# A down projection of seven half-size block products in place of eight

## The chip, the cores and the metric

One core of a Trainium2 chip runs one layer of a transformer-like trunk for 512 tokens. The metric is the time of the kernel on the device, in microseconds (us). Engines are named by what they do and by their short names in the profile: TensorE (PE, with PEld for its weight loads), VectorE (DVE), ScalarE (ACT), GpSimd (POOL) and SyncE (SP, which here issues nearly all DMAs).

## The reference, cut to what matters

```python
D_MODEL = 1024; SEQ = 512; D_FF = 2816
...
def conv_ffn(h, w_up, conv_w, conv_b, w_down):
    up = causal_dwconv(h @ w_up, conv_w, conv_b)
    g, val = jnp.split(up, 2, axis=-1)
    return (jax.nn.gelu(g) * val) @ w_down
...
        h = rms_norm(x, g[0])
        y = hybrid_mixer(h, ...)
        x = x + rms_norm(y, g[1])
        h = rms_norm(x, g[2])
        mem_n = rms_norm(mem, g[4])
        y = cross_attention(h, mem_n, xa_wq[l], xa_wkv[l], xa_wo[l])
        x = x + rms_norm(y, g[3])
        h = rms_norm(x, g[5])
        y = conv_ffn(h, ffn_w_up[l], ffn_conv_w[l], ffn_conv_b[l], ffn_w_down[l])
        x = x + rms_norm(y, g[6])
```

All data are float32. The change concerns the last matrix product, `[512, 2816] @ [2816, 1024]`, called the down projection, the norm and the residual behind it, and some work that is moved far ahead of it.

## The kernel before

The stages follow each other on TensorE: `va`/`sv`/`win` (input projections, with the branches' small work between them), `gate` and `br` (gates and branches, 32 units), `mo` (mix), `kT` and `v` (keys and values of the cross attention), `q`, `sc`, `pT`, `oT` (attention), `wo`, `up` (44 units) and `dn` (the down projection). In the names of the profile a matmul's output is one of these.

**Numbers.** Every operand of a large product is split into a high part (`F32R`, ScalarE's copy) and a low part (VectorE's subtraction), and `mm3` (line 123) makes of each product three matmuls of 128 rows by 128 stationary columns by up to 512 moving columns: high by high, high by low, low by high.

**Weights.** `plan` is the list of all weight units of 128 x 1024 (512 KB) in the order in which they are used. `load_unit` (line 68) issues the DMA on SP into a `raw` buffer, ScalarE makes `whi`, VectorE makes `wlo`; each of the three has four buffers that are used in turn. `unit()` (line 100) hands out the next unit and loads two further ones in the program's order.

**Slots.** All other large tiles are slots of 128 x 512 (2 KB of each partition), 70 in all. `get` takes the slot at the front of a list of free ones, `put` gives slots back at the list's end. So a slot is used again after all those that were free before it.

**Order.** The program is written in a program order; a planner (the tile framework) then orders each engine's instructions with that order as priority, and puts in the waits. On one engine instructions run in the planner's order.

**PSUM.** Eight banks of 128 x 512 float32: two with tag A, four B, two C, each tag used in turn.

**Up.** For each `f` of 22 the units `f` and `22+f` are made in A banks (the first two pairs in B banks), `up_post` runs the convolution along the tokens (one ScalarE and two VectorE instructions), `gate_up` (line 961) the gelu and the product, and splits the result into the pair `g[f]` (`gh`, `gl`) of 128 features x 512 tokens.

**Down.** `tok_unit` takes a weight unit, which holds two features' blocks (`k = 2i`, `2i+1`) of one half of the output columns, and four token tiles `t` of 128 tokens: the tokens' `g` is the stationary operand, the weights move. First come the left 512 output columns for all four tiles (11 units, B banks), then the right 512 for tiles 0 and 1 (A banks), then again the 11 units for tiles 2 and 3 (C banks); the last two units of each such pass are held back so that tile after tile ends. `down_post` (line 992) takes the sum of squares by ScalarE and multiplies by the gain on VectorE, both from PSUM; `finish` (line 999) takes the root and its reciprocal, multiplies, adds the residual `xt` and stores the tile's two halves.

**The stages into which work is moved.** The gates' loop makes for each of 4 branches and 8 output blocks `m` a gate (24 matmuls) and a branch's block (6 matmuls); the `kT` loop has 8 units of 24 matmuls of 256 columns; after `m == 6` in program order `turn2` transposes the normed residual.

Of the kernel before, what the change touches and what calls it, by code (L numbers as in the profile page):

```python
# [16 lines left out]
P = 128  # L17
S = 512
D = 1024
KT = D // P  # L20
# [18 lines left out]
def tile_trunk(ctx: ExitStack, tc: tile.TileContext, a: dict, out: bass.AP):  # L39
# [3 lines left out]
    wp = ctx.enter_context(tc.tile_pool(name="wp", bufs=1))  # L43
    tp = ctx.enter_context(tc.tile_pool(name="tp", bufs=2))
    pp = ctx.enter_context(tc.tile_pool(name="pp", bufs=1, space=PSUM))

    scalar, vector, gpsimd, tensor, sync = nc.scalar, nc.vector, nc.gpsimd, nc.tensor, nc.sync

# [4 lines left out]
    def get(name, dt=F32):  # L53
        i = free.pop(0)
        serial[0] += 1
        t = sp.tile([P, S], dt, tag=f"s{i}", name=f"{name}_{serial[0]}")
        held[id(t)] = (i, t)
        return t

    def put(*ts):  # L60
        for t in ts:
            free.append(held.pop(id(t))[0])

    def bank(tag, name):
        serial[0] += 1
        return pp.tile([P, S], F32, tag=tag, bufs={"A": 2, "B": 4, "C": 2}[tag], name=f"{name}_{serial[0]}")
# [13 lines left out]
    plan = [(a["w_in"][i], 1024) for i in range(18)]  # L80
# [8 lines left out]
    for f in range(2, NF):  # L89
        plan += [(a["w_up"][f], 1024), (a["w_up"][NF + f], 1024)]  # L90
    NP = NF // 2
    for c in (0, 1, 1):
        plan += [(a["w_down"][c * NP + i], 1024) for i in range(NP)]
    loaded, taken = [], [0]

    def prefetch(n):
        while len(loaded) < min(taken[0] + n, len(plan)):
            loaded.append(load_unit(*plan[len(loaded)]))

    def unit(ahead=LOOK):  # L100
        prefetch(1 + ahead)
        taken[0] += 1
        return loaded[taken[0] - 1]
# [19 lines left out]
    def mm3(ps, w, x, first, last):  # L123
        tensor.matmul(ps, lhsT=w[0], rhs=x[0], start=first, stop=False)  # L124
        tensor.matmul(ps, lhsT=w[0], rhs=x[1], start=False, stop=False)  # L125
        tensor.matmul(ps, lhsT=w[1], rhs=x[0], start=False, stop=last)  # L126
# [3 lines left out]
    def pump():  # L130
        if fibers:
            try:
                next(fibers[0])
            except StopIteration:
                fibers.pop(0)

    def drain():
        while fibers:
            pump()

    def dense(ps, wu, xs, width=P, base=0, first=True, last=True, tok=None):
        tok = slice(0, xs[0][0].shape[1]) if tok is None else tok
        n = len(xs)
        for k, (xh, xl) in enumerate(xs):
            c = base + k * width
            mm3(ps, wu(c, c + width), (xh[:, tok], xl[:, tok]), first and k == 0, last and k == n - 1)
            pump()

    def split(src, name, free_src=False):
        hi, lo = get(name + "h", F32R), get(name + "l", F32R)  # L150
        scalar.copy(hi, src)
        vector.tensor_tensor(lo, src, hi.bitcast(F32), op=ALU.subtract)
        if free_src:
            put(src)
        return hi, lo
# [70 lines left out]
    x = [get(f"x{k}") for k in range(KT)]  # L226
# [14 lines left out]
    for k in range(KT):  # L241
# [9 lines left out]
        hi, lo = get("xgh", F32R), get("xgl", F32R)  # L251
# [12 lines left out]
        c = slice((k % 2) * 256, (k % 2 + 1) * 256)  # L264
        sh, sl = svw[-1][0][:, c], svw[-1][1][:, c]
# [16 lines left out]
    for t in range(2):  # L282
        c = slice((t % 2) * 256, (t % 2 + 1) * 256)
# [307 lines left out]
    for p in R2:  # L591
        ps = w_in("B")
# [7 lines left out]
    for p in R2:  # L600
        ps = w_in()
# [7 lines left out]
    for p in R2:  # L609
        vector.tensor_mul(sc[p], sc[p], rb0s)  # L610
        ps = w_in()
# [6 lines left out]
    for p in R2:  # L618
        ps = w_in()
        vector.tensor_tensor(sc[p], ps, sc[p], op=ALU.mult)  # L620
        y[0][p] = split(sc[p], "ya", True)
    for p in R2:
        r = normed(w_in(), "r")
# [4 lines left out]
        gl_r.append(sg)  # L628


    acc = [None] * KT
    merged = []
    for ki, kb in enumerate(order):
        for m in range(KT):
            if m % 4 == 0:
                wb = unit()
            wg = unit()
            gp = bank("A", "gate")
            dense(gp, wg, xg)
            if kb == 1:  # L640
                drain()
            bp = bank("C", "br")
            dense(bp, wb, y[kb], base=(m % 4) * 256)
            sg = normed(gp, "sg")
            scalar.activation(sg, sg, AF.Sigmoid, bias=pc("bgate", kb * KT + m))
            vector.tensor_tensor(sg, bp, sg, op=ALU.mult)
            if ki == 0:
                acc[m] = sg
            else:
                vector.tensor_add(acc[m], acc[m], sg)  # L650
                put(sg)
                if ki == 3:
                    merged.append(split(acc[m], "mg", True))
        for p in range(2):
            put(*y[kb][p])
# [20 lines left out]
    LO, HI = slice(0, 256), slice(256, S)  # L676
    HALF = (slice(0, S), slice(S, D))
    T4 = range(4)
# [41 lines left out]
    g1 = gains(1)  # L720
    n1, n2 = TokNorm("n1"), TokNorm("n2")
    yt = [[None, None] for _ in T4]
    for c in range(2):
        ps = [bank("B" if c == 0 else "AACC"[t], "mo") for t in T4]
# [40 lines left out]
    for m in range(KT):  # L765
        ps = bank("A", "kT")
        dense(ps[:, 0:256], unit(), memk)
        c = slice((m % 2) * 256, (m % 2 + 1) * 256)
        hi, lo = kk[m // 2]
        scalar.copy(hi[:, c], ps[:, 0:256])  # L770
        vector.tensor_tensor(lo[:, c], ps[:, 0:256], hi[:, c].bitcast(F32), op=ALU.subtract)
        if m == 6:
            turn2(range(4), "BBBB")
    vv = [[None] * 2 for _ in range(2)]
    for cb in range(2):
        ps = [bank("B", "v") for _ in range(2)]
        for kp in range(4):
            wu = unit()
            for t in range(2):
                for i in range(2):  # L780
                    k = 2 * kp + i
                    tt = slice(t * P, (t + 1) * P)
# [95 lines left out]
    ps = [bank("AACC"[t], "wo") for t in T4]  # L878
# [58 lines left out]
    for t in T4:  # L937
        ps = bank("B", "wo")
# [22 lines left out]
    def gate_up(cg, cv):  # L961
        scalar.activation(cg, cg, AF.Gelu_apprx_tanh)
        vector.tensor_mul(cg, cg, cv)
        put(cv)
        return split(cg, "g", True)

    ups = [bank("B", "up") for _ in js]
    for tok in (LO, HI):
# [8 lines left out]
    g = [None] * NF  # L977
    for f in range(2, NF):
        cg = up(f)
        cv = up(NF + f)  # L980
        g[f] = gate_up(cg, cv)
        if f in (3, 5):
            i = f - 3
            cg, cv = up_post(js[i], ups[i]), up_post(js[i + 1], ups[i + 1])
            g[f // 2 - 1] = gate_up(cg, cv)
    for t in h3:
        put(*t)

    g6 = gains(6)
    n5 = TokNorm("n5")  # L990

    def down_post(ps, t, c):
        n5.square(ps, t, c)
        if c == 1:
            n5.add(t, t + 1)
        yt[t][c] = get("yt")
        vector.tensor_tensor(yt[t][c], ps, g6[c], op=ALU.mult)

    def finish(t):
        n5.root(t, t + 1)  # L1000
        for c in range(2):
            vector.scalar_tensor_tensor(yt[t][c], yt[t][c], n5.col(t), xt[t][c], op0=ALU.mult, op1=ALU.add)
            sync.dma_start(out[t][:, HALF[c]], yt[t][c])
        put(*yt[t])

    ps = [bank("B", "dn") for _ in range(4)]
    for fp in range(NP):
        tok_unit(ps, g, T4, fp, unit())
    for t in range(4):
        down_post(ps[t], t, 0)  # L1010
        if t == 0:
            scalar.activation(warm, n5.ss[:, 0:1], AF.Sqrt, scale=0.0, bias=epsc)
    for ts, tag in (((0, 1), "A"), ((2, 3), "C")):
        ps = {t: bank(tag, "dn") for t in ts}
        wus = []
        for fp in range(NP):
            wus.append(unit(3 if fp < NP - 2 else 2))
            if fp < NP - 2:
                tok_unit(ps, g, ts, fp, wus[-1])
        for t in ts:  # L1020
            for fp in (NP - 2, NP - 1):
                tok_unit(ps, g, (t,), fp, wus[fp])
            down_post(ps[t], t, 1)
            finish(t)


def _layout(inp):
# [76 lines left out]
```

## Time and profile before

| | us |
|---|---|
| median of 3 runs | 950.88 |
| range of the runs | 950.06 to 951.64 |
| profiled execution, time | 950.79 |
| profiled execution, span of the trace | 949.1 |
| TensorE busy in the span | 937.4 |
| VectorE busy | 535.1 |
| ScalarE busy | 422.6 |

How to read the profile: "busy" is the time in which an engine runs at least one instruction; a matmul's duration in the trace is longer than the distance between two starts, since matmuls are pipelined. A group's row names the line in the kernel, the engine, the operation, output and inputs with their shapes and types, and the count. In the timeline the first column is the start, the second the duration of the row's (merged) instructions, and the square bracket the idle time of the engine before it with what ended that. A row of a table of stretches has the busy time and the instruction count of each engine in that stretch, then the granted TensorE clock, the share of the DMA engines, and their GB/s. DMA issues have the count, the size of one, and the median time from issue to landing.

### The profile page before, as it was taken

The numbers are of one execution on the slowest core, as the hardware profiler recorded it, in microseconds if no ns is written. First come the engines' busy times: TensorE is split into PE (matmuls) and PEld (weight loads), VectorE is DVE, ScalarE is ACT, GpSimd is POOL, SyncE is SP. The second block draws the span as 40 slices with busy tenths as digits, with TensorE's granted clock in tenths as the row PEclk, the third lists the DMA queues.
The fourth block names the chain that finished last, engine by engine and source line by source line (L and its number), as shares of the span: only waits on it lengthen the run. The fifth ranks groups of instructions, "written<-read, shape, count | busy, mean of one in ns | idle before, by whom it ended". The sixth has DMA issues, their size and how long they took to land.

```text
span 949.1 us, 11692 instructions
## 1 busy us (share of the span) xinstructions
PE 937.4 (99%) x4600; PEld 789.0 (83%) x4600; DVE 535.1 (56%) x772; ACT 422.6 (45%) x651; POOL 8.2 (1%) x29
## 2 busy tenths in 40 slices
PE   7999999999999999999999999999999999999997
PEld 7888888888888888889888889988888888888885
DVE  5877567535454657466545745576565566622563
ACT  7836336423233534365434657444444444411542
POOL 1100000000000000000000000000000000000000
PEclk9999999999999999999999999999999999999999
DMA  9432221232344353326523420223223223333461
GB/s 324 148 126 89 67 92 64 91 100 77 110 133 146 99 189 100 120 88 194 173 73 98 141 69 2 89 89 102 97 89 112 89 93 107 105 99 108 154 229 61
DMA packets 34935, 107.68 MB, mean 113 GB/s; under 512 B 4657, under 2 KB 5569, under 8 KB 34881
## 3 DMA queue, kind: packets, MB, share of 16 engines
q1 hardware_dynamic: 34704, 106.92, 34.4%
q8 instruction: 36, 0.59, 0.3%
q14 instruction: 19, 0.15, 0.0%
q0 software_dynamic: 32, 0.02, 0.0%
q10 hardware_dynamic: 144, 0.00, 0.0%
HBM read 104.83 MB, written 2.10 MB: 113 GB/s over the span
## 4 chain that ended last, share of the span: by engine, by line
PE 96%; ACT 2%; DVE 1%; DMA 0%; issue 0%; SPq 0%; DVEq 0%; ACTq 0%
PE up L124 8%; PE up L125 8%; PE up L126 8%; PE gate L124 6%; PE gate L125 6%; PE gate L126 6%; PE dn L124 4%; PE dn L126 4%; PE dn L125 4%; PE win L124 4%; PE win L126 3%; PE win L125 3%; PE br L124 2%; PE q L124 2%; PE mo L124 2%; PE q L126 2%
## 5 line engine op out<-in xcount | busy, mean ns | idle before, releaser
L75 DVE TENSOR_TENSOR wlo<-raw,whi 128x1024 fp32r<-128x1024 f32 x170 | 207.8, 1224 | 214.8 <-ACT whi L74 214.2
L74 ACT CAST whi<-raw 128x1024 fp32r<-128x1024 f32 x170 | 178.7, 1052 | 323.7 <-issue 100.2
L124 PE MATMUL up<-h3h,whi 128*128 128x512 f32 (+1 forms) x368 | 138.1, 375 | 0.0
L125 PE MATMUL up<-h3l,whi 128*128 128x512 f32 (+1 forms) x368 | 138.1, 375 | 0.0
L126 PE MATMUL up<-h3h,wlo 128*128 128x512 f32 (+1 forms) x368 | 138.1, 375 | 0.0
L124 PE MATMUL gate<-xgh,whi 128*128 128x512 f32 x256 | 99.9, 390 | 0.0
L126 PE MATMUL gate<-xgh,wlo 128*128 128x512 f32 x256 | 99.7, 389 | 0.0
L125 PE MATMUL gate<-xgl,whi 128*128 128x512 f32 x256 | 99.6, 389 | 0.0
L124 PEld LDWEIGHTS up<-h3h,whi 128*128 128x128 f32 x368 | 69.3, 188 | 12.6
L126 PEld LDWEIGHTS up<-h3h,wlo 128*128 128x128 f32 x368 | 69.3, 188 | 12.6
L125 PEld LDWEIGHTS up<-h3l,whi 128*128 128x128 f32 x368 | 69.3, 188 | 12.3
L352 DVE TENSOR_TENSOR sg<-gate,rb0s 128x512 f32<-128x512 f32 x32 | 22.1, 692 | 83.8 <-PE gate L126 83.8
L124 PE MATMUL dn<-whi,gh 128*128 128x512 f32 x176 | 68.5, 389 | 0.0
L125 PE MATMUL dn<-wlo,gh 128*128 128x512 f32 x176 | 68.5, 389 | 0.0
L126 PE MATMUL dn<-whi,gl 128*128 128x512 f32 x176 | 68.5, 389 | 0.0
L546 DVE SCALAR_TENSOR_TENSOR c<-up,par,c 128x511 f32<-128x511 f32 (+1 forms) x88 | 65.1, 746 | 1.3
L124 PE MATMUL win<-xgh,whi 128*128 128x512 f32 x144 | 57.2, 397 | 0.0
L124 PEld LDWEIGHTS gate<-xgh,whi 128*128 128x128 f32 x256 | 48.1, 188 | 10.0
L126 PEld LDWEIGHTS gate<-xgh,wlo 128*128 128x128 f32 x256 | 48.1, 188 | 10.0
L126 PE MATMUL win<-xgh,wlo 128*128 128x512 f32 x144 | 56.3, 391 | 0.0
L125 PEld LDWEIGHTS gate<-xgl,whi 128*128 128x128 f32 x256 | 48.1, 188 | 9.8
L125 PE MATMUL win<-xgl,whi 128*128 128x512 f32 x144 | 56.1, 390 | 0.0
(337 smaller groups left out, 1557.5 us busy)
## 6 DMA issues: line engine op xcount, KB each, us to landing
raw<-in_w_up SPq DMA_DIRECT2D x44, 512.0 KB, 3.4
raw<-in_w_down SPq DMA_DIRECT2D x33, 512.0 KB, 3.5
raw<-in_w_gate SPq DMA_DIRECT2D x32, 512.0 KB, 3.4
raw<-in_w_in SPq DMA_DIRECT2D x18, 512.0 KB, 3.7
raw<-in_w_br SPq DMA_DIRECT2D x8, 512.0 KB, 3.4
raw<-in_w_mix SPq DMA_DIRECT2D x8, 512.0 KB, 3.5
raw<-in_w_k SPq DMA_DIRECT2D x8, 512.0 KB, 3.4
raw<-in_w_v SPq DMA_DIRECT2D x8, 512.0 KB, 3.5
```

What stands on the lines that cost most here:

```text
L74: scalar.copy(hi[:, :n], raw[:, :n])
L75: vector.tensor_tensor(lo[:, :n], raw[:, :n], hi[:, :n].bitcast(F32), op=ALU.subtract)
L124: tensor.matmul(ps, lhsT=w[0], rhs=x[0], start=first, stop=False)
L125: tensor.matmul(ps, lhsT=w[0], rhs=x[1], start=False, stop=False)
L126: tensor.matmul(ps, lhsT=w[1], rhs=x[0], start=False, stop=last)
L352: vector.tensor_tensor(t, ps, rb0s, op=ALU.mult)
L546: vector.scalar_tensor_tensor(dst[:, s:S], src[:, 0:S - s], pc(wname, (taps - 1 - s) * stride + off), dst[:, s:S], op0=ALU.mult, op1=ALU.add)
```

## The change

The left operand (tokens x features) and `w_down` are cut into 2 x 2 blocks: tokens 0 to 255 (`LO`) and 256 to 511 (`HI`); features of even and odd `k`; output columns 0 to 511 and 512 to 1023. The eight products of blocks become seven, p1 to p7, of sums and differences of blocks (Winograd's form); the result's blocks are sums and differences of the seven.

- *Sums of weights.* `sums_load(i)` loads four quarters of 128 x 512 by DMAs on the queue of GpSimd (POOL), `sums(i)` makes four sums of them on VectorE and stores them in `wsum`, a tile in DRAM, by four DMAs of POOL. There are 11 pairs `i`: nine in the gates' loop (a load at every third `m` from the sixth, its sums two `m` later) and two in the `kT` loop.
- *Weight plan.* The down stage now uses 33 units of 512 KB and 11 of 256 KB, 22 of the large ones from `wsum`.
- *Operands from the tokens' side.* `gate_up` no longer splits. `pair_up(i)` splits the `LO` tokens of two `g` into one pair of tiles (`gh`, `gl`) and makes differences in place; `second_a(i)` and `second_b(i)` make and split further operands in the down stage.
- *Down.* First half: for each pair `i` p1 (B), p2 (B), p6 (C), p5 (A), each with two token tiles and six matmuls per pair (one `mm3` a tile); the last two pairs are held back and finished product after product. Second half: p3 (B), p7 (B), p4 (C) in the same way.
- *Combining.* The results are built in `yt`, `d0` and `d1` in SBUF; `down_post` now works on these, with the gain's multiplication in place.

```diff
+    dp = ctx.enter_context(tc.tile_pool(name="dp", bufs=1, space=bass.MemoryType.DRAM))
...
-    for c in (0, 1, 1):
-        plan += [(a["w_down"][c * NP + i], 1024) for i in range(NP)]
+    wsum = dp.tile([2 * NP, P, 1024], F32, name="wsum")
+    for i in range(NP):
+        plan += [(a["w_down"][i], 1024), (wsum[i], 1024)]
+    for i in range(NP):
+        plan += [(a["w_down"][NP + i][:, S:2 * S], S), (wsum[NP + i], 1024)]
...
+    def sums_load(i):
+        q = [[get("wq") for _ in R2] for _ in R2]
+        for r in R2:
+            for c in R2:
+                gpsimd.dma_start(q[r][c], a["w_down"][c * NP + i][:, r * S:(r + 1) * S])
+        quarters[i] = q
+
+    def sums(i):
+        (b11, b12), (b21, b22) = quarters.pop(i)
+        vector.tensor_add(b11, b11, b12)
+        vector.tensor_add(b12, b12, b22)
+        vector.tensor_add(b22, b22, b11)
+        vector.tensor_add(b21, b21, b22)
+        gpsimd.dma_start(wsum[i][:, 0:S], b11)
+        gpsimd.dma_start(wsum[i][:, S:2 * S], b22)
+        gpsimd.dma_start(wsum[NP + i][:, 0:S], b21)
+        gpsimd.dma_start(wsum[NP + i][:, S:2 * S], b12)
+        put(b11, b12, b21, b22)
...
+            step = ki * KT + m - 5
+            if step >= 0 and step % 3 == 0:
+                sums_load(step // 3)
+            if step >= 2 and step % 3 == 2:
+                sums(step // 3)
...
+        if m in (2, 4):
+            sums(8 + m // 2)
+        if m in (0, 2):
+            sums_load(9 + m // 2)
...
-        return split(cg, "g", True)
+        return cg
+
+    def pair_up(i):
+        g0, g1 = g[2 * i], g[2 * i + 1]
+        hi, lo = get("gh", F32R), get("gl", F32R)
+        for j, t in enumerate((g0, g1)):
+            c = slice(j * 256, (j + 1) * 256)
+            scalar.copy(hi[:, c], t[:, LO])
+            vector.tensor_tensor(lo[:, c], t[:, LO], hi[:, c].bitcast(F32), op=ALU.subtract)
+        vector.tensor_sub(g1[:, LO], g0[:, LO], g1[:, LO])
+        vector.tensor_sub(g0[:, LO], g0[:, LO], g0[:, HI])
+        vector.tensor_sub(g0[:, HI], g1[:, HI], g0[:, HI])
+        vector.tensor_add(g1[:, LO], g1[:, LO], g0[:, HI])
+        gp1[i] = (hi, lo)
...
+            if f == 5:
+                pair_up(0)
+        if f % 2 == 1:
+            pair_up(f // 2)
...
-    def down_post(ps, t, c):
-        n5.square(ps, t, c)
-        if c == 1:
+    def down_post(t, c):
+        n5.square(yt[t][c], t, c)
+        if c == (1 if t < 2 else 0):
             n5.add(t, t + 1)
-        yt[t][c] = get("yt")
-        vector.tensor_tensor(yt[t][c], ps, g6[c], op=ALU.mult)
+        vector.tensor_tensor(yt[t][c], yt[t][c], g6[c], op=ALU.mult)
...
+    def product(ps, x, off, w, first, last, ts=(0, 1)):
         for t in ts:
+            tt = slice(off + t * P, off + (t + 1) * P)
+            mm3(ps[t], (x[0][:, tt], x[1][:, tt]), w, first, last)
+
+    def second_a(i):
+        g0, g1 = g[2 * i], g[2 * i + 1]
+        r = get("r2")
+        hi, lo = get("sh", F32R), get("sl", F32R)
+        vector.tensor_add(r[:, HI], g0[:, LO], g1[:, HI])
+        scalar.copy(hi[:, LO], g0[:, HI])
+        scalar.copy(hi[:, HI], r[:, HI])
+        vector.tensor_sub(lo[:, LO], g0[:, HI], hi[:, LO].bitcast(F32))
+        vector.tensor_sub(lo[:, HI], r[:, HI], hi[:, HI].bitcast(F32))
...
+    p1, p2, p6, p5 = ([bank(tag, "dn") for _ in T2] for tag in "BBCA")
+    second_a(0)
+    held_a = []
+    for i in range(NP):
+        wa, ws = unit(), unit()
+        if i + 1 < NP:
+            second_a(i + 1)
+        f, l = i == 0, i == NP - 1
+        todo = [(p1, gp1[i], 0, wa(0, S), f, l), (p2, gp1[i], 256, wa(S, 2 * S), f, l),
+                (p6, ops[i], 256, ws(S, 2 * S), f, l), (p5, ops[i], 0, ws(0, S), f, l)]
...
+    for n in range(4):
+        for t in T2:
+            for todo in held_a:
+                product(*todo[n], ts=(t,))
+        for t in T2:
+            if n == 0:
+                yt[t][0] = get("yt")
+                scalar.copy(yt[t][0], p1[t])
+            elif n == 2:
+                vector.tensor_sub(d0[t], p6[t], yt[t][0])
+                vector.tensor_add(yt[t][0], yt[t][0], p2[t])
+                down_post(t, 0)
...
+            elif n == 3:
+                vector.tensor_sub(d1[t], d0[t], p5[t])
+
+    def second_b(i):
+        g0, g1 = g[2 * i], g[2 * i + 1]
+        ah, al = get("sh", F32R), get("sl", F32R)
+        bh, bl = get("sh", F32R), get("sl", F32R)
+        scalar.copy(ah, g1)
+        vector.tensor_sub(al, g1, ah.bitcast(F32))
+        scalar.copy(bh[:, LO], g0[:, LO])
+        vector.tensor_sub(bl[:, LO], g0[:, LO], bh[:, LO].bitcast(F32))
...
+        wb, wz = unit(), unit()
...
+        todo = [(p3, ga, 0, wb(0, S), f, l), (p7, gb, 0, wz(S, 2 * S), f, l), (p4, ga, 256, wz(0, S), f, l)]
...
+    for n in range(3):
+        for t in T2:
+            for todo in held_b:
+                product(*todo[n], ts=(t,))
+            if n == 0:
+                yt[t][1] = get("yt")
+                vector.tensor_sub(yt[t][1], d1[t], p3[t])
+                down_post(t, 1)
+                finish(t)
+            elif n == 1:
+                yt[t + 2][1] = d1[t]
+                vector.tensor_sub(d1[t], d1[t], p7[t])
+                vector.scalar_tensor_tensor(d0[t], d0[t], -1.0, p7[t], op0=ALU.mult, op1=ALU.add)
+                down_post(t + 2, 1)
+            else:
+                yt[t + 2][0] = d0[t]
+                vector.tensor_add(d0[t], d0[t], p4[t])
+                down_post(t + 2, 0)
+                finish(t + 2)
```

More of the change, by code (lines that the diff above doesn't have):

```diff
@@ L628, in tile_trunk @@
         gl_r.append(sg)
+    quarters = {}
+    def sums_load(i):
[15 more added lines that the diff above has]
+        put(b11, b12, b21, b22)
     acc = [None] * KT
@@ L964, in gate_up @@
         put(cv)
-        return split(cg, "g", True)
+        return cg
+    gp1 = [None] * NP
+    def pair_up(i):
[10 more added lines that the diff above has]
+        gp1[i] = (hi, lo)
     ups = [bank("B", "up") for _ in js]
@@ L1004, in finish @@
         put(*yt[t])
[L1006 to L1019, printed above, removed]
-        for t in ts:
[L1021 to L1024, printed above, removed]
+    def product(ps, x, off, w, first, last, ts=(0, 1)):
+        for t in ts:
+            tt = slice(off + t * P, off + (t + 1) * P)
+            mm3(ps[t], (x[0][:, tt], x[1][:, tt]), w, first, last)
@@ new lines, in tile_trunk @@
+    T2 = (0, 1)
+    ops = {}
+    def second_a(i):
[7 more added lines that the diff above has]
+        vector.tensor_sub(lo[:, HI], r[:, HI], hi[:, HI].bitcast(F32))
+        put(r)
+        ops[i] = (hi, lo)
@@ new lines, in tile_trunk @@
+    p1, p2, p6, p5 = ([bank(tag, "dn") for _ in T2] for tag in "BBCA")
[8 more added lines that the diff above has]
+                (p6, ops[i], 256, ws(S, 2 * S), f, l), (p5, ops[i], 0, ws(0, S), f, l)]
+        if i < NP - 2:
+            for p in todo:
+                product(*p)
+            put(*gp1[i], *ops.pop(i))
+        else:
+            held_a.append(todo)
@@ new lines, in tile_trunk @@
+    d0, d1 = [get("d0") for _ in T2], [get("d1") for _ in T2]
+    for n in range(4):
[10 more added lines that the diff above has]
+                down_post(t, 0)
+                if t == 0:
+                    scalar.activation(warm, n5.ss[:, 0:1], AF.Sqrt, scale=0.0, bias=epsc)
+            elif n == 3:
+                vector.tensor_sub(d1[t], d0[t], p5[t])
@@ new lines, in tile_trunk @@
+    for i in (NP - 2, NP - 1):
+        put(*gp1[i], *ops.pop(i))
+    def second_b(i):
[6 more added lines that the diff above has]
+        vector.tensor_sub(bl[:, LO], g0[:, LO], bh[:, LO].bitcast(F32))
+        put(g0, g1)
+        ops[i] = (ah, al), (bh, bl)
+    p3, p7, p4 = ([bank(tag, "dn") for _ in T2] for tag in "BBC")
@@ new lines, in tile_trunk @@
+    second_b(0)
+    held_b = []
+    for i in range(NP):
+        wb, wz = unit(), unit()
+        if i + 1 < NP:
+            second_b(i + 1)
+        f, l = i == 0, i == NP - 1
+        ga, gb = ops[i]
+        todo = [(p3, ga, 0, wb(0, S), f, l), (p7, gb, 0, wz(S, 2 * S), f, l), (p4, ga, 256, wz(0, S), f, l)]
+        if i < NP - 2:
+            for p in todo:
+                product(*p)
+            put(*ga, *gb)
+        else:
+            held_b.append(todo)
+    for n in range(3):
[12 more added lines that the diff above has]
+                down_post(t + 2, 1)
+            else:
+                yt[t + 2][0] = d0[t]
+                vector.tensor_add(d0[t], d0[t], p4[t])
+                down_post(t + 2, 0)
+                finish(t + 2)
```

## The prediction

> **What bounds the kernel now.** I read the page first (span, busy shares, chain), then the tile `dn`, the stretches of the stages that the edit touches, and the timeline of the end.
>
> ```profile
> span 949.1 us, 11692 instructions
> PE 937.4 (99%) x4600; PEld 789.0 (83%) x4600; DVE 535.1 (56%) x772; ACT 422.6 (45%) x651; POOL 8.2 (1%) x29
> ...
> PE 96%; ACT 2%; DVE 1%; DMA 0%; issue 0%; SPq 0%; DVEq 0%; ACTq 0%
> ...
> L75 DVE TENSOR_TENSOR wlo<-raw,whi 128x1024 fp32r<-128x1024 f32 x170 | 207.8, 1224 | 214.8 <-ACT whi L74 214.2
> L74 ACT CAST whi<-raw 128x1024 fp32r<-128x1024 f32 x170 | 178.7, 1052 | 323.7 <-issue 100.2
> ```
>
> ```profile
> L124 PE MATMUL dn<-whi,gh x176: 389/389/389, 823.0 to 942.0; 128*128 128x512 f32 x176
> ...
> L126 PE MATMUL dn<-whi,gl x176: 388/389/389, 823.4 to 942.4; 128*128 128x512 f32 x176
> ```
>
> ```profile
> core 0: us, PE busy (x) PEld busy (x) DVE busy (x) ACT busy (x) POOL busy (x), PEclk, DMA share, GB/s
> 165.00:370.00 205.00, 205.00 (x910) 169.96 (x909) 106.82 (x134) 69.38 (x89) 0.00 (x0) 1.00 0.37 118
> 371.50:411.00 39.50, 39.50 (x178) 32.74 (x177) 19.06 (x27) 15.13 (x24) 0.00 (x0) 1.00 0.33 107
> 411.00:436.00 25.00, 24.89 (x190) 23.54 (x189) 22.59 (x36) 19.28 (x46) 0.00 (x0) 1.00 0.37 126
> 609.00:822.00 213.00, 213.00 (x941) 176.40 (x940) 136.15 (x167) 96.30 (x124) 0.00 (x0) 1.00 0.31 101
> 823.00:877.00 54.00, 54.00 (x240) 44.72 (x239) 15.05 (x14) 11.78 (x12) 0.00 (x0) 1.00 0.32 106
> 877.00:936.00 59.00, 59.00 (x262) 48.87 (x261) 31.12 (x34) 26.83 (x36) 0.00 (x0) 1.00 0.50 162
> ```
>
> The chain is TensorE for 96%, and in gates, mix, up and down it has no gap. So the kernel is TensorE from end to end, and a matmul less is worth its interval, not its modelled duration of 389 ns. In `dn` the 528 matmuls start from 823.0 to 942.4: 119.4/527 = 0.2266 us apart, at a granted clock of 1.00. VectorE, at 56%, is busiest in 411 to 436: 22.59 of 25.
>
> **What the change removes.** Each product is 2 token tiles x 11 pairs x 3 matmuls of the same form (128x512) = 66; seven are 462 for 528. Gain 66 x 0.2266 = 14.96 us.
>
> **The end.** What follows the last matmul grows. Before:
>
> ```profile
> 881.82 1.29 DVE L997 TENSOR_TENSOR yt<-dn,gain 128x512 f32<-128x512 f32 x2 [1.35 <-ACT sq L693]
> ...
> 942.41 0.39 PE L126 MATMUL dn<-whi,gl 128*128 128x512 f32 x1
> 942.48 3.71 SPq L1003 DMA_DIRECT2D out_y<-yt  x4
> 942.83 0.60 ACT L693 ACTIVATE sq<-dn 128x512 f32<-128x512 f32 x1 [1.51 <-PE dn L126]
> 943.33 0.19 ACT L693 ACTIVATION_READ_ACCUMULATOR sq<-dn 128x1 f32 x1
> 943.55 0.16 DVE L697 TENSOR_TENSOR rs_n<-ss_n 128x1 f32<-128x1 f32 x1 [0.44 <-ACT sq L693]
> 943.63 0.69 DVE L997 TENSOR_TENSOR yt<-dn,gain 128x512 f32<-128x512 f32 x1
> 943.75 0.29 ACT L701 ACTIVATE rs_n<-rs_n,epsc 128x1 f32<-128x1 f32 x1 [0.23 <-DVE rs_n L697]
> 944.23 0.15 DVE L702 RECIPROCAL rs_n<-rs_n 128x1 f32<-128x1 f32 x1
> 944.42 1.41 DVE L1002 SCALAR_TENSOR_TENSOR yt<-yt,rs_n,xt 128x512 f32<-128x512 f32 x2
> ```
>
> ```profile
> 418.48 5.39 DVE L740 SCALAR_TENSOR_TENSOR xt<-yt,rs_n,xt 128x512 f32<-128x512 f32 x8
> ```
>
> The last matmul ends at T = 942.80, VectorE at 945.83 (T+3.03), the span at 949.1. VectorE's instructions overlap: two tensor_tensor of 0.69 take 1.29, the second starting 0.60 after the first; eight scalar_tensor_tensor take 5.39, 0.67 each. After: products p3, p7, p4 finish in six groups of six matmuls (1.36 us), so p3's first tile ends at T-6.80. All combining now falls behind that point: p3: per tile subtract, gain, add, root's reciprocal, two residuals; p7: two combines and gain; p4: as p3. Counted: 12 tensor_tensor x 0.605 = 7.26; 10 scalar_tensor_tensor x 0.674 = 6.74; 4 adds x 0.08 (943.55 to 943.63) and 4 reciprocals x 0.19 (944.23 to 944.42) = 1.08. Together 15.1 us for one engine, with 6.8 us of matmul above it. It doesn't start at T-6.8: the last weight unit's buffer comes free at T-8.16 (four units back), its cast (1.05) and subtract (1.22) run until T-5.9. From there 15.1 gives T+9.2, against T+3.03: cost 6.2 us; the output DMA follows as before. Bounds: from T-6.8 with the small ones hidden in between, T+7.5, cost 4.5; with full durations (0.69, 0.74) and 1 us of waiting for ScalarE's squares, which the in-place gain multiply must now wait for, cost 9.
>
> At one place the Trainium skill speaks against this: "VectorE: DVE Perf Modes", The DRAIN you can't avoid, says that the next op does not start until the pipe empties. By that the 12 and 10 count full; that is a rival below. The rows above (1.29 for two) disagree with it.
>
> **The start of the down stage.** In program order pair 0's second operands (`second_a(0)`) stand behind `pair_up(10)`, which needs the last up result:
>
> ```profile
> 819.72 1.53 DVE L546 SCALAR_TENSOR_TENSOR c<-up,par,c 128x511 f32<-128x511 f32 x2
> 824.01 1.23 DVE L75 TENSOR_TENSOR wlo<-raw,whi 128x1024 fp32r<-128x1024 f32 x1 [2.77 <-ACT whi L74]
> 825.16 1.53 DVE L546 SCALAR_TENSOR_TENSOR c<-up,par,c 128x511 f32<-128x511 f32 x2
> 826.72 0.69 DVE L963 TENSOR_TENSOR c<-c,c 128x512 f32<-128x512 f32 x1
> ```
>
> ```profile
> L771 DVE TENSOR_TENSOR kl<-kT,kh x8: 414/418/424, 423.8 to 443.9; 128x256 fp32r<-128x256 f32 x8
> ```
>
> In that order: 827.4 + 6 x 0.42 (pair_up) + 3 x 0.42 = 831.2; p6 needs them at 823.0 + 12 x 0.2266 = 825.7: a wait of 5.5 us. But the order on the engines is not the program's:
>
> ```profile
> L124 PE MATMUL kT<-memh,whi x64: 278/283/387, 415.3 to 441.3; 128*128 128x256 f32 x64
> ...
> 421.02 3.34 PE L755 MATMUL h2T<-ident,xt 128*128 128x128 f32 x24
> ...
> L124 PE MATMUL gate<-xgh,whi x256: 389/389/501, 147.7 to 369.2; 128*128 128x512 f32 x128
> ...
> 347.40 1.71 SPq L719 DMA_DIRECT2D xt<-in_x_rows  x2
> ```
>
> The `h2T` transposes, written behind seven of the eight `kT` units, began 5.7 us into `kT`'s 26, and `xt`, written behind the gates (which last to 369), was loaded at 347: whatever is ready is put where its engine would idle. `second_a(0)` needs only pair 0, done long before, and three slots. Slots come out of a list in the order in which they went back; behind the two of the gains stand `h3`'s, first tile first, and the last up unit has read that first tile some 5 us before it ends (24 matmuls of 0.2266). VectorE is idle between 821.25 and 824.0, which holds 3 x 0.42. I take 0, keep 0 to 5.5.
>
> **The middle.** p7 of pair 0 reads `wsum`'s first unit, whose buffers are those of `ws` of pair 9, free 0.68 us before the first half ends; 1.05 + 1.22 later it is 1.6 to 1.9 after it, where it is wanted after p3's 1.36. Take 0.5; 0 if pair 1's p3 is put between, 2.5 if both `d1` subtracts go first.
>
> **Work that TensorE hides.** Down, per pair: VectorE 2 x 1.22 + 3 x 0.42 = 3.7 of 24 x 0.2266 = 5.44, later 1.22 + 0.6 + 0.6 + 0.42 = 2.9 of 4.08; ScalarE less. 1 MB per 5.44 us is 193 GB/s, against 162 over 877 to 936. Up: `pair_up` for two splits adds 6 x 0.42 - 2 x 0.6 = 1.3 us per pair to 136 of 213. If this cover went, each would cost its length.
>
> **The sums.** 11 x 4 adds x 0.6 = 26.6 us of VectorE, 44 loads and 44 stores of 256 KB on POOL's queue, which is otherwise empty by then. Nine stand in the gates, where VectorE has 98 us free; their 18.9 MB in 27 units of 6.8 us (30 x 0.2266) add 103 GB/s to 118. The DMA price is not shown for POOL; the nearest rows:
>
> ```profile
> xt<-in_x_rows SPq DMA_DIRECT2D x8, 256.0 KB, 3.3
> row<-in_x_rows SPq DMA_DIRECT2D x8, 256.0 KB, 5.4
> walpha<-in_w_alpha POOLq DMA_DIRECT2D x1, 16.0 KB, 3.9
> ...
> 2.02 0.61 POOL L329 DMA_DIRECT2D walpha<-in_w_alpha  x1
> ```
>
> Four loads issued 0.61 apart and landing in 3.3 to 5.4 are there after 7.2 at most; the adds stand 13.6 us behind. The stores wait for the adds on POOL's queue and hold only the next sum's loads; SP waits for them first at the down stage's `wsum` loads, 300 us and more later, and the weights queued behind those then wait for nothing new. A gain is excluded: TensorE has no gap there. I take 0. Sums 9 and 10 stand in `kT`, where VectorE has 2.4 us of 25 left; they cost up to 8 x 0.6 = 4.8 us there, nothing if drawn forward into the mix stage (19.06 of 39.5 busy). That hangs on their slots: at `kT` 46 of 70 are in the list, and counted back 46 returns the next four are the sources of `mem`, then the squares of the mix's first half, both free before 400; so the loads, and the adds with them, can come early. Take 0.5.
>
> **Sum.** -14.96 + 6.2 + 0 + 0.5 + 0 + 0.5 = -7.8, against this execution's 950.79: 943.0; the median lies 0.09 above, so 943.1.
>
> **Rivals.**
> (a) Program order holds VectorE at the start, in `kT` and in the middle: 3 to 6 us more, 946 to 949. For it: those chains are real. Against: the drawn-forward rows.
> (b) VectorE's durations add up without overlap: 12 x 0.69 + 10 x 0.74 + 8 x 0.15 = 16.9, cost 8.0, time 944.9. Against: 1.29 for two.
> (c) Slower: the adds wait in VectorE's strict order for POOL's loads, and gates' results and weight splits wait behind them. Were four loads to run one after another at 5.4, they take 21.6 against 13.6; of the 8.0 over, the second PSUM bank for gates covers one unit of 6.8, leaving 1.2 x 11 = 13 us: 956. It decides from (7.8 + 1.9)/11 = 0.9 us of lost TensorE time per sum. For it: gates, sums and stores meet on the same DMA engines. The Trainium skill's "DMA: Bandwidth & Descriptors", Issuing engines are not separate DMA queues, says that such transfers interleave whoever starts them; no run here shows POOL and SP together. Against: DMA share 0.37 there.
> (d) It saves nothing because products wait for operands: needs 15 us in 120; VectorE's 3.7 of 5.44 speaks against.
>
> **How the numbers follow.** Forecast 0.62; (a) 0.14; (b) 0.08; (c) 0.09; (d) or a milder (c), no change, 0.07. About 0.2% (1.9 us) is what can be told from no change. Faster 0.84, within 0.07, slower 0.09. The range takes the end's bounds (4.5 to 9), the small terms from 0 to 2, and (a): 940 to 949, leaving out (c) and (d), 0.16, and a little below.
>
> **What would show it.** 462 `dn` matmuls, 0.2266 apart; first `dn` start unchanged near 823 (later means the sums cost); no TensorE gap at p6 of pair 0 and under 1 us at p3/p7; VectorE solid from about T-6 to T+9, then the span's end 3.3 after it. Wrong if TensorE's busy share falls in the gates or `kT`, or VectorE waits there for POOL's loads.

## The result, and the profile after

| | us |
|---|---|
| before, median | 950.97 |
| after, median (941.37 to 943.08) | 942.47 |
| ratio after to before, 95% interval | 0.991 (0.9898 to 0.9922) |
| profiled execution after, time and span | 941.86, 940.0 |

The kernel is 8.5 us faster; 943.1 was forecast. The page of the changed kernel (span, busy time by engine, chain by engine, and the issues of the new DMAs with their size and the time to landing):

```profile
span 940.0 us, 12070 instructions
PE 922.4 (98%) x4534; PEld 776.9 (83%) x4534; DVE 606.7 (65%) x940; ACT 441.1 (47%) x707; POOL 56.0 (6%) x117
...
PE 94%; DVE 3%; ACT 2%; DMA 0%; issue 0%; SPq 0%; DVEq 0%; ACTq 0%
...
wq<-in_w_down POOLq DMA_DIRECT2D x44, 256.0 KB, 3.9
wsum<-wq POOLq DMA_DIRECT2D x44, 256.0 KB, 3.3
```

TensorE's busy time fell by 15.0 us, VectorE's rose by 71.6, and VectorE now holds 3% of the chain where it held 1%: the end. The stretches of the same stages:

```profile
165.00:370.00 205.00, 205.00 (x910) 169.92 (x910) 120.42 (x159) 70.59 (x89) 24.98 (x46) 1.00 0.54 180
371.50:411.00 39.50, 39.50 (x175) 32.67 (x174) 24.21 (x36) 14.82 (x24) 8.68 (x16) 1.00 0.64 214
411.00:436.00 25.00, 24.89 (x191) 23.61 (x190) 22.29 (x36) 19.61 (x45) 0.00 (x0) 1.00 0.39 126
609.00:822.00 213.00, 213.00 (x941) 176.42 (x940) 146.85 (x212) 93.02 (x128) 0.00 (x0) 1.00 0.31 103
823.00:877.00 54.00, 54.00 (x240) 44.74 (x239) 42.29 (x68) 33.26 (x54) 0.00 (x0) 1.00 0.59 181
```

TensorE still fills each of them. VectorE has 13.6 us more in the gates, 5.2 more in the mix stage (371.5 to 411) and no more in `kT` (411 to 436). The planner began the sums early: the first load is issued at 90.7, the first of the nine sums is done and the second begun when the gates begin at 147.3, and the ninth is done by 307. The down stage, by the tile `dn`, and VectorE's timeline behind it:

```profile
L130 PE MATMUL dn<-whi,sl x110: 388/389/389, 825.6 to 926.9; 128*128 128x512 f32 x110
L128 PE MATMUL dn<-whi,gh x44: 389/389/389, 822.5 to 876.2; 128*128 128x512 f32 x44
```

```profile
921.44 1.28 DVE L1149 TENSOR_TENSOR yt<-d,dn 128x512 f32<-128x512 f32 x2
...
928.83 0.68 DVE L1154 TENSOR_TENSOR d<-d,dn 128x512 f32<-128x512 f32 x1
929.43 0.68 DVE L1155 SCALAR_TENSOR_TENSOR d<-d,dn 128x512 f32<-128x512 f32 x1
930.03 0.68 DVE L1159 TENSOR_TENSOR d<-d,dn 128x512 f32<-128x512 f32 x1
...
933.57 2.74 DVE L1055 SCALAR_TENSOR_TENSOR d<-d,rs_n,xt 128x512 f32<-128x512 f32 x4
```

The 462 matmuls start from 822.45 to 926.95: 104.5/461 = 0.2267 us apart, so no gap at p6, none in the middle. With 0.39 for the last one the end of the last matmul, T, is 927.34. VectorE's combining starts at 921.44 = T-5.9 and ends at 936.31 = T+8.97, in an almost unbroken row; the span ends 3.7 later, at 940.0.

So the spans, 949.1 and 940.0, differ thus: the down stage's matmuls, first start to last, 119.45 to 104.5, -14.95; from the last matmul's end to the span's end 6.3 to 12.66, +6.4; and the first `dn` matmul at 822.45 in place of 822.96, -0.5, which stands already in the first stage (see e4). The stages between are as long as before: from the first to the last start the gates take 222.0 us, mix 43.4, `kT` 26.2 and up 242.5 in both profiles.

### The profile page after: what moved, and what is told of

Same layout as the page of the kernel before. It is cut to its first block, busy times and chain, and to the rows that moved or that the text cites. A ratio compares the mean times of both kernels' runs of the same rounds, so it can differ in the third digit from the quotient of the medians.

```text
span 940.0 us, 12070 instructions
## 1 busy us (share of the span) xinstructions
PE 922.4 (98%) x4534; PEld 776.9 (83%) x4534; DVE 606.7 (65%) x940; ACT 441.1 (47%) x707; POOL 56.0 (6%) x117
## 4 chain that ended last, share of the span: by engine, by line
PE 94%; DVE 3%; ACT 2%; DMA 0%; issue 0%; SPq 0%; DVEq 0%; ACTq 0%
PE up L130 8%; PE up L128 8%; PE up L129 8%; PE gate L128 6%; PE gate L129 6%; PE gate L130 6%; PE win L128 4%; PE win L129 3%; PE win L130 3%; PE dn L129 3%; PE dn L128 3%; PE dn L130 3%; PE br L128 2%; PE mo L128 2%; PE q L128 2%; PE q L130 2%
## 5 line engine op out<-in xcount | busy, mean ns | idle before, releaser
L76 DVE TENSOR_TENSOR wlo<-raw,whi 128x1024 fp32r<-128x1024 f32 (+1 forms) x181 | 214.3, 1189 | 155.5 <-ACT whi L75 155.0
L75 ACT CAST whi<-raw 128x1024 fp32r<-128x1024 f32 (+1 forms) x181 | 185.1, 1026 | 276.0 <-issue 78.9
L128 PE MATMUL dn<-whi,sh 128*128 128x512 f32 x110 | 42.8, 389 | 0.0
L129 PE MATMUL dn<-wlo,sh 128*128 128x512 f32 x110 | 42.8, 389 | 0.0
L130 PE MATMUL dn<-whi,sl 128*128 128x512 f32 x110 | 42.8, 389 | 0.0
```

The lines of the kernel that those rows point to most:

```text
L75: scalar.copy(hi[:, :n], raw[:, :n])
L76: vector.tensor_tensor(lo[:, :n], raw[:, :n], hi[:, :n].bitcast(F32), op=ALU.subtract)
```

## The experiments

Theory 1: a product is worth 66 matmul intervals, the sums are hidden, and what is paid back is VectorE's queue behind the last matmul. The rivals: the sums cost something that another gain hides; the end is a chain of latencies, not a queue; VectorE's operands become the bound. The medians, each with the ratio to the kernel before that ran beside it (950.6 to 951.6 there, so a difference of less than 1 us between two rows is not read):

| run | us | ratio (95%) |
|---|---|---|
| e1 sums alone, eight products | 951.0 | 1.0 (0.9991 to 1.0008) |
| e2 six gain multiplications left out | 939.73 | 0.9879 (0.9866 to 0.9893) |
| e3 six products | 928.01 | 0.9759 (0.9746 to 0.9772) |
| e4 p3 first | 938.12 | 0.9861 (0.9846 to 0.9876) |
| e5 the gates' sums made twice | 975.4 | 1.0253 (1.0232 to 1.0274) |
| e6 late slots for sums 9 and 10 | 944.77 | 0.9929 (0.9915 to 0.9944) |
| e7 sums on SP's queue | 942.98 | 0.9908 (0.9891 to 0.9924) |
| e8 p3 first, four pairs held | 938.14 | 0.9859 (0.9844 to 0.9874) |
| e9 VectorE's part doubled | 944.85 | 0.9941 (0.9927 to 0.9956) |
| e11 further transfers alone | 952.84 | 1.0027 (1.0018 to 1.0037) |
| e12 p3 first, last tile ahead | 938.1 | 0.9873 (0.9856 to 0.9889) |
| e13 fewer slots in the gates | 942.26 | 0.9908 (0.9891 to 0.9924) |

**e1: the sums without the products.** The kernel before, with `sums_load` and `sums` at the same places, and the down stage as it was.

> The kernel before (eight products) with the sums added as in the change: 44 loads, 44 adds and 44 stores into wsum, which nothing reads here. Theory 1 (the sums are wholly hidden; the change is 66 matmul intervals less, paid back by a longer end on VectorE): same as before within 0.3%, 951.0, with TensorE's stages starting within 0.3 us of those of the kernel before, counted from the first win matmul. Rival A (the sums cost some us and the down stage gains correspondingly more than counted): slower, 952 to 956, with a stage (gates, mix or kT) visibly longer.

The time is that of the kernel before, within 0.9 us either way. TensorE's gates, by the first and the last start, in the changed kernel and then in e1, and e1's stretch:

```profile
L128 PE MATMUL gate<-xgh,whi x256: 389/389/501, 147.3 to 368.8; 128*128 128x512 f32 x128
```

```profile
L126 PE MATMUL gate<-xgh,whi x256: 388/389/502, 148.3 to 369.9; 128*128 128x512 f32 x128
...
165.00:370.00 205.00, 205.00 (x910) 169.98 (x910) 120.97 (x159) 70.44 (x89) 25.57 (x48) 1.00 0.53 181
```

221.5 us in the changed kernel, as in the kernel before (147.7 to 369.2), and 221.6 in e1, where TensorE is busy in 205.00 of 205 with the sums' VectorE and POOL work beside it. Mix, `kT` and up last 43.4, 26.2 and 242.5 us in e1 too. Rival A falls: the sums cost nothing here.

**e2: the end is a queue, with some latency in it.**

```diff
-        vector.tensor_tensor(yt[t][c], yt[t][c], g6[c], op=ALU.mult)
+        if gain:
+            vector.tensor_tensor(yt[t][c], yt[t][c], g6[c], op=ALU.mult)
```

> The changed kernel, with the six multiplications by the norm's gain of the second half left out (the other two stay), so that part of the output lacks the gain. Theory 1 (the end is VectorE's queue: what counts is the number of its instructions behind T-6.8): 6 x 0.605 = 3.6 us less, 938.8, VectorE done at about T+5.4. Rival B (the end is a chain of latencies: last product, square, root, reciprocal, residual; VectorE's load beside it has slack): at most the one multiplication in the chain, 0.6 us less, 941.9. If squares and roots partly set the end, between: 2 to 3 us.

2.7 us less than the changed kernel, between the two theories and nearer to the first. From its profile, the last matmul and VectorE's last rows:

```profile
L130 PE MATMUL dn<-whi,sl x110: 388/389/390, 824.8 to 926.2; 128*128 128x512 f32 x110
```

```profile
929.21 0.16 DVE L728 TENSOR_TENSOR rs_n<-ss_n 128x1 f32<-128x1 f32 x1 [0.19 <-ACT sq L724]
929.83 0.16 DVE L728 TENSOR_TENSOR rs_n<-ss_n 128x1 f32<-128x1 f32 x1 [0.45 <-ACT sq L724]
930.01 0.16 DVE L733 RECIPROCAL rs_n<-rs_n 128x1 f32<-128x1 f32 x1
...
931.73 1.42 DVE L1056 SCALAR_TENSOR_TENSOR d<-d,rs_n,xt 128x512 f32<-128x512 f32 x2
```

VectorE is done at 933.15 = T+6.6 in place of T+9.0: of 3.6 us taken away 2.4 came off, and in the brackets VectorE now waits for ScalarE's squares. So the queue was the bound, and some 2.4 us below it lies the chain of squares and roots.

**e3: the price of a product.** p5 is taken out of `todo` and of the held part; `d1` takes p6.

> The changed kernel with the product p5 left out (six products; d1 takes p6 in its place, so the left columns' combination is another one). Theory 1 (a product is worth 66 intervals of 0.2266 us as long as TensorE is the bound): 15.0 us less, 927.5; VectorE then has 3.7 of 4.08 us per pair in the first half. Rival C (operands and weight splits become the bound when the first half has 18 matmuls a pair): gaps on TensorE in the first half, 930 to 936.

14.5 us less for 66 matmuls. The first and the last start:

```profile
L130 PE MATMUL dn<-whi,sl x88: 388/389/398, 826.2 to 913.5; 128*128 128x512 f32 x88
L128 PE MATMUL dn<-whi,gh x44: 389/389/390, 823.0 to 865.1; 128*128 128x512 f32 x44
```

90.5 us for 395 intervals that at 0.2266 take 89.5: 1.0 us of waiting appears with 18 matmuls a pair, and VectorE is busy in 35.8 of the first 36 us (823 to 859). So seven products are not yet limited by operands; six begin to be.

**e4: the same products, combined earlier.** In the second half p3 runs over all pairs before p7 and p4; three pairs of p7 and p4 are held back.

```diff
-        plan += [(a["w_down"][NP + i][:, S:2 * S], S), (wsum[NP + i], 1024)]
+    for i in range(0, NP, 2):
+        plan += [([a["w_down"][NP + k][:, S:2 * S] for k in range(i, min(i + 2, NP))], min(2, NP - i) * S)]
+    for i in range(NP):
+        plan += [(wsum[NP + i], 1024)]
...
+    for i in range(NP):
+        if i % 2 == 0:
+            wb = unit()
...
+        product(p3, ga[i], 0, wb(c, c + S), i == 0, i == NP - 1)
+    for t in T2:
+        yt[t][1] = get("yt")
+        vector.tensor_sub(yt[t][1], d1[t], p3[t])
+        down_post(t, 1)
+        finish(t)
...
+        todo = [(p7, gb[i], 0, wz(S, 2 * S), f, l), (p4, ga[i], 256, wz(0, S), f, l)]
```

> The same seven products in another order: in the second half p3 runs over all 11 pairs first (its weights two pairs to a unit), its combining and the store of tiles 0 and 1 then lie under p7 and p4, of which the last three pairs are held back. Same number of matmuls. Theory 1: after the last matmul stands only p4's second tile and some of the first: VectorE done at about T+4.2 in place of T+9.0, so 4.8 us less, 937.7. Rival B (chain of latencies): the chain behind the last matmul is the same, so 942.5 stays within 0.5 us. Against both: if the three held pairs or the paired units starve TensorE, a gap of up to 2 us there.

4.4 us less than the changed kernel. From its profile:

```profile
L136 PE MATMUL dn<-whi,sl x110: 388/389/390, 827.4 to 928.8; 128*128 128x512 f32 x110
L134 PE MATMUL dn<-whi,gh x44: 388/389/390, 824.3 to 878.0; 128*128 128x512 f32 x44
```

```profile
928.78 0.69 DVE L1056 TENSOR_TENSOR d<-d,gain 128x512 f32<-128x512 f32 x1
929.38 0.16 DVE L739 RECIPROCAL rs_n<-rs_n 128x1 f32<-128x1 f32 x1
929.46 0.67 DVE L1179 TENSOR_TENSOR d<-d,dn 128x512 f32<-128x512 f32 x1
930.04 1.41 DVE L1061 SCALAR_TENSOR_TENSOR d<-d,rs_n,xt 128x512 f32<-128x512 f32 x2
...
932.23 1.42 DVE L1061 SCALAR_TENSOR_TENSOR d<-d,rs_n,xt 128x512 f32<-128x512 f32 x2
```

The down stage is again 104.5 us long, without a gap, and VectorE ends at 933.65 = T+4.5. The same matmuls and the same VectorE work, only less of it behind the last matmul: this shows the end to be a matter of what stands there. (The first `dn` matmul starts at 824.3 here and at 821.7 in e2: the first stage, `va`, which waits for the first loads, starts its last matmul at 25.5 us here and at 22.9 in e2, and the whole trace is shifted by that. So the ends are compared from T.)

**e8 and e12: further at the end.** e8 holds four pairs and writes the gain's product to a tile of its own; e12 holds three and sets the last tile's combination ahead (`tc.high_priority()` for the tile of `t == 1`).

> The order with p3 first, and four pairs held back in place of three, and the gain's product written to a tile of its own, so that it need not wait for the square that reads the tile. Theory 1: the first tile of p4 is then done with before the last matmul, so the end is one tile's chain: T+3.8 in place of T+4.5: 937.4 (0.7 less than with three held). Rival F: four held pairs use all four weight buffers, and TensorE waits for the last unit's split, 0.3 to 1.5 us: 938 to 939.

> The order with p3 first and three pairs held back, the gain's product in a tile of its own, and the combining of the last tile put ahead of the residual of the tile before it (four held pairs had gained nothing: the planner set the last tile's addition behind that residual). Theory 1: VectorE still has about 4.2 us of work behind the last matmul, so T+4.2 in place of T+4.5: 937.8, at most 0.4 less than with p3 first alone, hardly to be told from it. Rival: the last tile's chain alone, T+3.5: 937.1.

938.14 and 938.1: neither is to be told from e4. VectorE ended at T+4.4 and T+4.3. In e8 the planner put the last tile's addition behind the residual of the tile before, which ate the gain; in e12 the order is as wanted, but about 4 us of VectorE work still stand behind T, as expected.

**e6: cover that hangs on slots.**

```diff
+        if m == 0:
+            for _ in range(len(free) - 8):
+                free.append(free.pop(0))
```

> The changed kernel with the list of free slots turned before the loads of sums 9 and 10, so that they get slots which are read until 424 (the residual's) and can't be drawn forward into the mix stage. Theory 1 (what keeps them free of cost is only that their slots are free early): the adds fall into or behind the kT stage, where VectorE has 22.3 of 25 us busy, and TensorE waits for it up to 4.8 us: 944 to 947, with the gap between 424 and 442. Rival D (VectorE's load there doesn't set TensorE's pace, or the planner puts them behind into the v stage): 942.5 within 0.2%.

2.3 us slower than the changed kernel (1.8 by the ratios), inside what theory 1 gave. First, where POOL issued those loads and stores in the changed kernel:

```profile
375.96 0.54 POOL L641 DMA_DIRECT2D wq<-in_w_down  x1 [68.92 <-DVE mem L701]
...
382.33 0.55 POOL L650 DMA_DIRECT2D wsum<-wq  x1 [1.20 <-DVE wq L646]
...
390.20 0.54 POOL L641 DMA_DIRECT2D wq<-in_w_down  x1 [1.44 <-ACT sq L724]
```

They waited for the last reader of `mem`'s source and for the mix's squares, as counted in the prediction, and ran in the mix stage. In e6 (who waited for whom on TensorE, and `kT`'s first and last start):

```profile
PE kT L128 <- DVE kl L809: 2.1, 1, 2.1
```

```profile
L128 PE MATMUL kT<-memh,whi x64: 278/283/387, 415.5 to 444.1; 128*128 128x256 f32 x64
```

`kT` takes 28.6 us there by these rows, 26.0 before, and the other stages from the gates to `dn` are as long as in the changed kernel. 4.8 us of VectorE work cost 2.6 once it fell where VectorE was full.

**e7: the queue.** The sums' 88 DMAs issued by `sync` in place of `gpsimd`.

> The changed kernel with the sums' 44 loads and 44 stores on SP's queue in place of POOL's, among the weights' loads. Theory 1 holds the queue to matter: a store waits for VectorE's add and the weight loads issued behind it wait too, but weights are loaded up to four units (20 us) ahead, so it costs 0 to 2 us: 942.5 to 944.5. Rival E (an in-order queue with stores in it starves the weights): 946 to 955, with TensorE gaps in the gates. Were it faster than 941.5, POOL's queue itself would have had a cost.

942.98 against 942.47, not to be told apart. The DMAs landed after 3.7 and 3.0 us (median) there, 3.9 and 3.3 on POOL. That which queue starts a transfer matters little agrees with the Trainium skill's "DMA: Bandwidth & Descriptors", Issuing engines are not separate DMA queues.

**e5, e9, e11, e13: how much more would be hidden?** e5 makes each sum of the gates twice. Its adds also stand one unit behind their loads in program order, in place of two, so the edit halves that lead as well:

> The changed kernel with each of the nine sums of the gates made twice (the second time with the same result): 36 more loads, adds and stores, in the same 27 units. Theory 1 (the sums lie under TensorE with room to spare: VectorE 120 of 205 us and DMA share 0.54 over 165 to 370): again no cost, 942.5 within 0.3%, DMA share in the gates up to 0.7. Rival A (the sums are at the edge of what the DMA engines and VectorE hide): 2 to 8 us slower, with TensorE gaps in the gates.

The forecast missed by far: 33 us slower, nearly all of it in the gates, which last from 147.8 to 401.5. VectorE's and TensorE's waits between 80 and 402, first in the changed kernel, then in e5 (us in all, times, longest):

```profile
DVE wq L646 <- DMA wq<-in_w_down: 19.3, 7, 6.5
...
DVE wq L647 <- DMA wq<-in_w_down: 12.3, 6, 3.6
```

```profile
DVE wq L646 <- DMA wq<-in_w_down: 42.3, 12, 5.1
...
DVE wq L647 <- DMA wq<-in_w_down: 20.5, 7, 4.8
...
DVE wq L649 <- DMA wq<-in_w_down: 15.9, 4, 5.2
...
PE gate L128 <- DVE sg L356: 17.5, 7, 4.9
```

VectorE stands at the sums for 79 us in place of 32, and TensorE for VectorE: rival (c) of the prediction, at twice the work and half the lead. One such place in e5, VectorE's rows and then TensorE's:

```profile
284.56 0.69 DVE L647 TENSOR_TENSOR wq<-wq,wq 128x512 f32<-128x512 f32 x1 [3.23 <-DMA wq<-in_w_down]
285.16 0.68 DVE L356 TENSOR_TENSOR sg<-gate,rb0s 128x512 f32<-128x512 f32 x1
```

```profile
285.99 0.77 PE L128 MATMUL gate<-xgh,whi 128*128 128x512 f32 x1 [3.53 <-DVE sg L356]
...
289.08 0.63 PE L130 MATMUL gate<-xgh,wlo 128*128 128x512 f32 x1
289.51 0.63 PE L128 MATMUL gate<-xgh,whi 128*128 128x512 f32 x1
```

From 147.8 to 402 TensorE is idle for 22.6 us (254.2 less 231.6 busy), 17.5 of them in front of VectorE's `sg`. The pauses also slow what follows: after the three longest (4.86, 3.53 and 3.83 us) 29 matmuls in all start about 0.43 us apart, as in the last two rows, in place of 0.2266, some 5 us more; after pauses of 3.15 us and less none does. The granted clock of the whole stretch is 0.97, for 1.00 in the changed kernel.

Already in the changed kernel VectorE waits there 32 us, and TensorE has no idle time in the gates. Three runs take e5 apart:

> After the sums made twice cost 33 us: what broke, VectorE's load, the DMA engines, or the waits of VectorE's strict order for loads? Here the changed kernel has four further VectorE instructions of the adds' size for each pair (on the four sums, leaving them as they are), and no further DMA. Theory 2 (VectorE's time is not the limit; what costs is VectorE standing at an add whose load has landed later than the order assumed): 942.5 within 0.3%, VectorE 135 of 205 us busy in the gates. Rival G (VectorE's load broke it): 8 to 20 us slower.

```diff
+        for t in (b11, b22, b21, b12):
+            vector.tensor_tensor(t, t, t, op=ALU.max)
```

944.85: the gates last 223.8 us for 221.5. The time lies inside theory 2's 0.3%, but the gates show that VectorE's part alone does cost 2.3 us: not 0, and far from the 8 to 20 of rival G.

> The changed kernel with eight further transfers of 256 KB per pair of the gates, from w_down to an unused DRAM tile, on POOL's queue behind the loads: nothing waits for them but the queue and the DMA engines; no slots, no adds. Theory 2: the loads of the sums land later than the order assumed (5 us and more in place of 3.9), VectorE waits for them in its strict order, and where a wait is longer than the gates' banks cover, TensorE waits: 5 to 30 us slower, VectorE's waits for wq grown to over 50 us. Rival H (in the run with the sums made twice it was the scarcity of slots, which made loads late): 942.5 to 945, waits as in the changed kernel.

This one doesn't answer the question. The transfers wait for nothing, so the planner drew all 72 of them ahead of the gates, from 3.4 us on, many to where the first weights are loaded (first 45 us of the changed kernel, then of e11):

```profile
0.00:45.00 45.00, 40.40 (x284) 36.99 (x285) 29.95 (x81) 36.58 (x75) 7.20 (x27) 1.00 0.68 238
```

```profile
0.00:45.00 45.00, 33.43 (x215) 31.04 (x215) 21.10 (x43) 26.73 (x62) 18.32 (x48) 0.92 0.95 335
```

The 10 us were lost there: the last matmul of `va` starts at 34.3 us, in place of 23.7, and the gates are as long as ever (157.9 to 379.4). That the time falls into the range of theory 2 is chance, since VectorE's waits for `wq` stay at 31 us. The run shows what POOL's transfers do where loads are the bound: the DMA share rose from 0.68 to 0.95, and the transfers of 264 KB of `w_vs` landed after 9.8 us (5.1 in the changed kernel), `w_in`'s units after 7.7 (3.9).

> What made the sums made twice cost 33 us? In that run a slot came round again after about 7 units of the gates (26 free slots, 3.7 returned per unit) in place of 11. Here the changed kernel with its sums made once keeps 10 slots idle through the gates, so that a slot also comes round after about 7 units (16 free, 2.3 per unit); DMA bytes and adds are as in the change. Theory 3 (loads issued only when a slot comes free, close before their adds, make VectorE wait in its strict order): 5 to 30 us slower, VectorE's waits for wq over 50 us in the gates. Rival I (it is the rate: twice the bytes landing later, together with twice the adds): within 0.3% of 942.5.

942.26: the scarcity of slots alone is not it; VectorE's waits for `wq` are 27 us, for 32 in the changed kernel. So neither VectorE's share alone (2.3 us) nor the slots explain e5's 33. What is left, alone or together, is the bytes (loads of `wq` landed after 5.1 us in place of 3.9), the lead of one unit in place of two, loads that stand on POOL's queue behind stores which wait for adds, and that in e5 the second store of a sum must wait for the first one to the same place. No run here parts these; this stays open.

## Why the prediction was right, point by point

- *66 intervals of 0.2266.* Right: -14.95 us measured, and 14.5 for the next product (e3).
- *The end.* Forecast: VectorE busy from T-5.9 to T+9.2, cost 6.2. Measured: T-5.9 to T+8.97, cost 5.9 on VectorE and 6.4 to the span's end, since the output landed 0.4 later behind it. e2 and e4 show the queue; e2 shows too that the bound below it, the chain over ScalarE, is closer than the count told. The lower bound was mis-added: -6.8 and 7.26 + 6.74 give T+7.2, not T+7.5; the forecast's time does not use it, and its range would move by 0.3. Rival (b), durations without overlap, falls by the rows above: starts 0.60 apart at durations of 0.68. The section of the Trainium skill that the prediction named against its count ("VectorE: DVE Perf Modes", The DRAIN you can't avoid) goes on that a next op that is not held starts earlier, which the prediction left out. The rows agree with that addition; from the rule without it the measurement differs, and decides.
- *The start, 0.* Right: no wait at p6, `dn` without a gap. Rival (a) did not occur; its chains were drawn forward: `second_a`'s first addition starts at 817.9, and the part of `pair_up(10)` that needs the last up result at 828.3.
- *The middle, 0.5.* 0 measured.
- *Work that TensorE hides.* Hidden, as forecast, with less room: VectorE was counted at 3.7 of 5.44 us a pair, and is busy in 42.29 of 54 us from 823 to 877, 4.3 a pair, with the last work of up in it.
- *The sums, 0 in the gates and 0.5 in `kT`.* 0 and 0 (e1). The slots were free when counted, and e6 shows the price where they aren't: 2.3 us. For (c) the forecast was right, but the reason it gave (loads there long before the adds) was not: on the engine the adds stand close behind their loads, and VectorE waits 32 us for them. None of that reaches TensorE; in e5, with twice the work and half the lead, much of it does. So the 0 in the gates came out with less to spare than was argued.
- *Left over.* 0.5 us of the profiled spans' difference is the first stage's, which moves by more than that between profiles (e2, e4).

The median lies 0.6 us below the forecast. In the profiled spans the forecast was 1.3 us too long: the two terms of 0.5 did not appear, the first stage was 0.5 shorter, and the end 0.2 longer than 6.2.

## What to carry to other kernels

Where one engine is the bound without a gap, count its instructions by the distance of their starts, and then count the work of the next engine that falls behind the last of them: here 15.0 us of matmuls were saved and 6.4 given back there. Combining earlier, with the same work, gave 4.4 of it back (938.1 us, e4, the best version here with its two variants). Work that is hidden elsewhere is hidden by something that can be named, here a slot that is free early; turn that one thing, as e6 does, to learn how much of it is left. e5 turned several at once, and so its cause stays open.

## What was not expected of the hardware

Twice the bytes and adds in the gates, at half the lead, took 33 us, though by the stretches VectorE had 85 of 205 us free and the DMA share stood at 0.54: the mean of a stage says little where an engine that runs its instructions in order waits for single transfers. After the pauses of over 3.5 us in e5 matmuls started 0.43 us apart for a while in place of 0.2266, so a long pause cost more than its length. And transfers of 256 KB that nothing needs, put beside the first loads, cost 10 us.
